# A binary cross-entropy kernel at the DMA limit: reordering VectorE's tail, and sixteen 32-byte writes to the output at launch

## The chip, the core and the metric

The kernel runs on one core of one Trainium2 chip. The metric is the device time of an execution in microseconds (us), as the median over executions. The profile's span is about 2 us shorter than this time (1865.4 against 1867.3 us in the profiled run of the kernel before).

## The reference

```python
pred   = uniform(0.01, 0.99), (8192, 8192), float32
target = 0 or 1,              (8192, 8192), float32
eps = 1e-7
pred = np.clip(pred, eps, 1 - eps)
return -(target * np.log(pred) + (1 - target) * np.log(1 - pred))
```

Two inputs of 268 MB are read and one output of 268 MB is written: 805.3 MB in all, with little work on each element. As target is 0 or 1, the kernel computes -ln|pred + target - 1|.

## The kernel before

The 8192 x 8192 elements are cut into chunks of 128 partitions x up to 15360 columns, two halves of a chunk at the start and at the end, and a last one of 2048 columns. Two rings in SBUF hold them: pred in float32 (in place also the result), target cast to bfloat16 by the load.

```python
def load(k):                       # target by GpSimd's queue, pred too (chunk 0: SP's)
    queue = nc.sync if k == 0 else nc.gpsimd
    nc.gpsimd.dma_start(out=spot(ring_t, k), in_=chunk(target, k))
    queue.dma_start(out=spot(ring_p, k), in_=chunk(pred, k))

def store(k):                      # the last three by SP's queue
    queue = nc.sync if k >= n - 3 else nc.gpsimd
    queue.dma_start(out=chunk(out, k), in_=spot(ring_p, k))

def front(k, *part):
    # VectorE: clip (L82), then (target - 1) + pred (L85); ScalarE: Abs (L88), Ln (L89)
    ...

def back(k, *part):                # VectorE: times -1 (L93)
    ...

# the main part
for k in range(3): load(k)
nc.vector.memset(warm, 1.0)
nc.scalar.activation(out=warm, in_=warm, func=Act.Ln)     # its table load: 1.28 us from 0.73 us
front(0); front(1); back(0); store(0); back(1); store(1); load(3)
for k in range(2, n - 3):
    front(k, (0, 2)); front(k, (1, 2)); back(k, (0, 2)); back(k, (1, 2))
    ...                                                   # store(k), further loads
store(n - 4)
a, b, c = n - 3, n - 2, n - 1      # 7680, 7680 and 2048 columns
front(a); front(b, (0, 2)); front(b, (1, 2))
back(a); store(a); front(c); back(b); store(b); back(c); store(c)
```

(Reformatted and cut; the "..." mark cuts.)

## Time and profile before

| | before |
|---|---|
| time, median of the first 3 runs | 1867.1 us (1866.34 to 1867.97) |
| span in the profile | 1865.4 us |
| busy: VectorE (DVE), ScalarE (ACT), GpSimd (POOL) | 60%, 48%, 3% |
| DMA queues, share of 16 engines | 98.4% and 1.7% |

Here the busy shares of compute tell little: nothing is above 60% but the DMA engines. So the reader should look at the stretches in which a DMA engine stands idle or is slow. Two views serve for this. The windows give each stretch's DMA share and GB/s. The trace's packet records give start, length, queue and bytes of each packet; they carry no engine number, but outside holes one packet starts as another ends, so the records can be threaded into 16 lanes (in the kernel before, 98 of 100 packets then start between 0.019 us before and 0.005 us after the end of the last one in their lane, and none more than 0.02 us before it; so records overlap a little). "An engine" below is such a lane. The prediction shows the lines.

### The profile page before, as it was taken

How to read it: one execution, taken by the hardware profiler on the slowest of the kernel's cores; microseconds unless marked ns; L12 is line 12 of the kernel's file. 1: busy time of each engine (PE TensorE's matmuls, PEld its weight loads, DVE VectorE, ACT ScalarE, POOL GpSimd, SP SyncE). 2: the span in 40 equal slices, each digit the busy share in tenths (PEclk: the TensorE clock that was granted, in tenths of full speed). 3: DMA queues.
4: the chain of work that ended last, by engine and by line, in shares of the span. 5: the costliest groups of instructions: out<-in, count | busy, mean ns of one | idle time of the engine just before them, and what ended most of it. 6: DMA issues, size and time to landing. Idle time of an engine off the chain costs nothing.

```text
span 1865.4 us, 619 instructions
## 1 busy us (share of the span) xinstructions
DVE 1122.2 (60%) x210; ACT 899.9 (48%) x142; POOL 60.9 (3%) x111
## 2 busy tenths in 40 slices
DVE  4655767555576655557665555766555576755575
ACT  3345553335555334555543355553345555433556
POOL 0000000000000000000000000000000000000010
DMA  9999999999999999999999999999999999999998
GB/s 295 376 358 340 357 341 365 387 379 353 344 353 353 359 387 381 351 353 345 353 360 387 385 350 353 345 353 361 383 386 349 354 350 345 362 383 387 356 329 379
DMA packets 15988, 671.13 MB, mean 360 GB/s; under 512 B 1776, under 2 KB 1776, under 8 KB 1904
## 3 DMA queue, kind: packets, MB, share of 16 engines
q0 software_dynamic: 15408, 658.25, 98.4%
q1 hardware_dynamic: 576, 12.85, 1.7%
q14 instruction: 4, 0.03, 0.0%
HBM read 536.87 MB, written 268.44 MB: 432 GB/s over the span
## 4 chain that ended last, share of the span: by engine, by line
DMA 36%; ACT 24%; issue 23%; DVE 16%; POOL 1%; DVEq 0%; POOLq 0%; PEldq 0%
DMA ring_p<-in_pred_dram 33%; ACT ring_p L88 12%; ACT ring_p L89 12%; DVE ring_p L85 8%; DVE ring_p L82 4%; DVE ring_p L93 4%; DMA out_dram<-ring_p 3%; POOL ring_t L73 0%; POOL out_dram L78 0%; DVEq L154 0%; POOLq L78 0%; DVEq L85 0%; PEldq L154 0%; POOLq L74 0%; POOLq L73 0%
## 5 line engine op out<-in xcount | busy, mean ns | idle before, releaser
L88 ACT ACTIVATE ring_p<-ring_p 128x7680 f32<-128x7680 f32 (+1 forms) x70 | 450.6, 6437 | 948.2 <-DVE ring_p L85 948.2
L85 DVE SCALAR_TENSOR_TENSOR ring_p<-ring_t,ring_p 128x7680 f32<-128x7680 bf16 (+1 forms) x70 | 557.2, 7960 | 2.4
L82 DVE TENSOR_SCALAR ring_p<-ring_p 128x7680 f32<-128x7680 f32 (+1 forms) x70 | 284.0, 4057 | 391.0 <-DMA ring_p<-in_pred_dram 391.0
L93 DVE TENSOR_SCALAR ring_p<-ring_p 128x7680 f32<-128x7680 f32 (+1 forms) x69 | 284.0, 4117 | 336.2 <-ACT ring_p L89 336.2
L89 ACT ACTIVATE ring_p<-ring_p 128x7680 f32<-128x7680 f32 (+1 forms) x70 | 451.1, 6444 | 2.2
L78 POOL DMA_DIRECT2D out_dram<-ring_p x34 | 21.6, 635 | 841.0 <-DVE ring_p L93 841.0
L74 POOL DMA_DIRECT2D ring_p<-in_pred_dram x36 | 19.3, 535 | 909.5 <-DMA out_dram<-ring_p 909.5
L73 POOL DMA_DIRECT2D ring_t<-in_target_dram x37 | 20.3, 550 | 0.8 <-PEq L154 0.8
L99 ACT ACT_TABLE_LOAD x1 | 1.3, 1283 | 0.7 <-PEq L143 0.7
L98 DVE MEMSET warm<- 1x8 f32 x1 | 0.1, 65 | 0.8 <-PEq L143 0.8
L99 ACT ACTIVATE warm<-warm 1x8 f32<-1x8 f32 x1 | 0.2, 208 | 0.0
L143 POOL MEMSET const-float32-0.0<- 128x1 f32 x1 | 0.1, 98 | 0.2 <-issue 0.2
L143 POOL MEMSET const-bfloat16-1.0<- 128x1 bf16 x1 | 0.1, 101 | 0.0
L143 POOL MEMSET const-float32-1.0<- 128x1 f32 x1 | 0.1, 98 | 0.0
L143 POOL MEMSET const-uint8-127<- 128x1 uint8 x1 | 0.1, 98 | 0.0
## 6 DMA issues: line engine op xcount, KB each, us to landing
ring_p<-in_pred_dram POOLq DMA_DIRECT2D x32, 7680.0 KB, 35.9
out_dram<-ring_p POOLq DMA_DIRECT2D x32, 7680.0 KB, 29.2
ring_t<-in_target_dram POOLq DMA_DIRECT2D x32, 3840.0 KB, 46.8
ring_p<-in_pred_dram POOLq DMA_DIRECT2D x3, 3840.0 KB, 35.0
ring_t<-in_target_dram POOLq DMA_DIRECT2D x4, 1920.0 KB, 27.6
out_dram<-ring_p POOLq DMA_DIRECT2D x2, 3840.0 KB, 27.6
out_dram<-ring_p SPq DMA_DIRECT2D x2, 3840.0 KB, 12.2
ring_p<-in_pred_dram SPq DMA_DIRECT2D x1, 3840.0 KB, 18.6
```

Of the source, the lines that this page charges most:

```text
L73: nc.gpsimd.dma_start(out=spot(ring_t, k), in_=chunk(target, k))
L74: queue.dma_start(out=spot(ring_p, k), in_=chunk(pred, k))
L78: queue.dma_start(out=chunk(out, k), in_=spot(ring_p, k))
L82: nc.vector.tensor_scalar(out=p, in0=p, scalar1=EPS, scalar2=1 - EPS, op0=Alu.max, op1=Alu.min)
L85: nc.vector.scalar_tensor_tensor(out=p, in0=t, scalar=1.0, in1=p, op0=Alu.subtract, op1=Alu.add)
L88: nc.scalar.activation(out=p, in_=p, func=Act.Abs)
L89: nc.scalar.activation(out=p, in_=p, func=Act.Ln)
L93: nc.vector.tensor_scalar(out=p, in0=p, scalar1=-1.0, scalar2=None, op0=Alu.mult)
L98: nc.vector.memset(warm, 1.0)
L99: nc.scalar.activation(out=warm, in_=warm, func=Act.Ln)
L143: nc = _bacc.Bacc("TRN2", target_bir_lowering=False, num_devices=1)
```

## The change

Its intent: on VectorE, put front(a) ahead of the last back of the chunk before (z), so that ScalarE does not wait for it (16.49 us in the trace); and write 16 runs of 32 bytes to the output at launch, meant as one for each DMA engine, so that a first write's cost, if there is one, is paid early.

```diff
-    warm = pool.tile([1, 8], fp32, name="warm", tag="warm")
+    warm = pool.tile([16, 8], fp32, name="warm", tag="warm")
...
+        nc.vector.memset(warm, 1.0)
+        nc.scalar.dma_start(out=chunk(out, 0)[0 : P : P // 16, : warm.shape[1]], in_=warm)
         for k in range(3):
             load(k)
-        nc.vector.memset(warm, 1.0)
...
-        for k in range(2, n - 3):
+        for k in range(2, n - 4):
...
-        store(n - 4)
-        a, b, c = n - 3, n - 2, n - 1
+        z, a, b, c = range(n - 4, n)
+        front(z, (0, 2))
+        front(z, (1, 2))
+        back(z, (0, 2))
         front(a)
+        back(z, (1, 2))
+        store(z)
         front(b, (0, 2))
```

(Blank lines and the rest of the loop are left out; its test of which stores to issue falls away.)

More of the change, by code (lines that the diff above doesn't have):

```diff
@@ L111 @@
             back(k, (1, 2))
-            if k < n - 4:
-                store(k)
-                for j in range(k + 2, n if k == n - 5 else k + 3):
-                    load(j)
-        store(n - 4)
-        a, b, c = n - 3, n - 2, n - 1
+            store(k)
+            for j in range(k + 2, n if k == n - 5 else k + 3):
+                load(j)
+        z, a, b, c = range(n - 4, n)
+        front(z, (0, 2))
+        front(z, (1, 2))
+        back(z, (0, 2))
         front(a)
+        back(z, (1, 2))
+        store(z)
         front(b, (0, 2))
```

## The prediction

> **What bounds the kernel now.** I read the page first: busy shares, the DMA row of the slices, and the queues.
>
> ```profile
> DVE 1122.2 (60%) x210; ACT 899.9 (48%) x142; POOL 60.9 (3%) x111
> ...
> DMA  9999999999999999999999999999999999999998
> ...
> q0 software_dynamic: 15408, 658.25, 98.4%
> q1 hardware_dynamic: 576, 12.85, 1.7%
> ...
> HBM read 536.87 MB, written 268.44 MB: 432 GB/s over the span
> ```
>
> No compute engine is above 60%, while the two DMA queues together fill the 16 engines' time (98.4% + 1.7%, a little over 100 because records overlap). So the DMA engines are the bound in every slice but the last, and the chain of waits, which names ACT (24%) and DVE (16%), does not contradict this: it follows releases, not capacity. The change moves no fewer bytes, so it can only gain where DMA engines stand idle or a packet takes longer than it should. I went through the trace's DMA packet records one by one. In the steady part a packet of 61440 bytes takes 2.267 us, so 16 engines give 16 x 61440 / 2.267 = 433.6 GB/s. All of the 805.3 MB at that rate is 1857.2 us, against a span of 1865.4 us. **Some 8 us is all that any reordering can address**, 0.44% of the time.
>
> Where are these 8 us? (1) Launch: the first packets start 1.74 to 2.49 us into the span, and the first on each engine takes 1.45 to 2.29 us where the next take 1.14 to 1.17. (2) At 72.6 to 73.4 us the last packet of the load ahead of the first store takes 2.80 to 3.49 us on all 16 engines, on average 0.97 us more than 2.267. The windows (columns: stretch, DVE, ACT, POOL, clock, DMA share, GB/s) show the rate drop there with the share still near 1:
>
> ```profile
> 70.00:72.50 2.50, 0.00 (x0) 0.00 (x0) 1.02 (x2) 1.00 0.91 393
> 72.50:76.00 3.50, 0.00 (x0) 0.00 (x0) 0.00 (x0) 1.00 0.99 307
> 76.00:80.00 4.00, 2.83 (x1) 0.00 (x0) 0.00 (x0) 1.00 1.05 453
> ```
>
> Later starts of a store cost only some engines 0.1 to 0.9 us. They pull the engines apart: one load's landings spread over 0.7 us at the start, 4.4 us from about 460 us on. (3) The tail. The timeline (start, length, what, idle before and its releaser):
>
> ```profile
> 1797.53 6.60 ACT L89 ACTIVATE ring_p<-ring_p 128x7680 f32<-128x7680 f32 x1
> 1804.17 4.16 DVE L93 TENSOR_SCALAR ring_p<-ring_p 128x7680 f32<-128x7680 f32 x1 [8.97 <-ACT ring_p L89]
> 1808.24 4.15 DVE L82 TENSOR_SCALAR ring_p<-ring_p 128x7680 f32<-128x7680 f32 x1
> 1808.62 3.90 POOL L78 DMA_DIRECT2D out_dram<-ring_p  x1 [22.23 <-DVE ring_p L93]
> 1812.43 8.16 DVE L85 SCALAR_TENSOR_TENSOR ring_p<-ring_t,ring_p 128x7680 f32<-128x7680 bf16 x1
> ...
> 1820.62 6.61 ACT L88 ACTIVATE ring_p<-ring_p 128x7680 f32<-128x7680 f32 x1 [16.49 <-DVE ring_p L85]
> ...
> 1838.08 14.93 SPq L78 DMA_DIRECT2D out_dram<-ring_p  x3
> ```
>
> DVE waits 8.97 us for ScalarE before back(z, second half), although chunk a is in SBUF by 1801.6 (its landing records). ScalarE then waits 16.49 us for front(a). Everything after is late: the store of b cannot be issued before its negation ends at 1851.51. The windows show what the DMA loses:
>
> ```profile
> 1844.00:1848.00 4.00, 0.65 (x1) 4.00 (x2) 0.00 (x0) 1.00 0.96 415
> 1848.00:1850.00 2.00, 2.00 (x1) 1.97 (x2) 0.00 (x0) 1.00 0.36 154
> 1850.00:1852.00 2.00, 2.00 (x2) 1.06 (x1) 0.00 (x0) 1.00 0.04 15
> 1852.00:1854.00 2.00, 0.65 (x1) 0.00 (x0) 0.00 (x0) 1.00 1.17 492
> ```
>
> Between 1848 and 1852.4 the engines run dry one after another: eight at 1848.1 to 1848.7, the last at 1851.5. All restart at 1852.4 and end together at 1864.0 to 1864.2. The gap is up to 4.4 us on the engines that are ahead, but **only 0.84 us on the engine that is behind**.
>
> [...]the issue at 1808.62 took 3.90 us instead of the usual 0.54 and ended 0.13 us after the tensor_scalar that ran over it.[...]
>
> **The change, part by part.**
>
> Part 1, the tail. I redo the timeline with the new order: front(z), back(z, first), front(a), back(z, second), store(z), front(b), back(a), store(a), front(c), back(b), store(b), back(c), store(c). Durations are from the timeline (7680 columns: tensor_scalar 4.16, subtract-add 8.16, each activation 6.6; half of it for 3840 columns: 2.15, 4.16, 3.4). front(a) starts at 1801.6 when a lands, and ends at 1801.6 + 12.4 = 1814.0, 6.6 us before 1820.6. back(z, second) follows to 1818.2, 9.9 us later than now, and store(z) is issued then. It must be: the loads of c end on the engines between 1820.3 and 1824.6, so store(z) still arrives in time, and no tensor_scalar covers its issue, as b lands only at 1819.8. ScalarE does a from 1814.1 to 1827.3 (before: 1820.6 to 1833.9). front(b) runs on DVE from 1819.8 to 1832.4; ScalarE does b from 1827.3 to 1840.9 (before: to 1847.3). back(a) ends at 1836.6, so store(a) goes out 1.4 us earlier; front(c) ends at 1840.1, back(b) at 1845.1 and store(b) goes out there, 6.4 us earlier than 1851.5. DMA needs it from 1848.1 at the earliest: the gap closes on all engines. But the end is the last engine's. The one that is behind gets 0.84 us back; those ahead finish some 4 us sooner, which nobody sees. **Part 1: -0.8 us**, though compute is 6.4 us earlier.
>
> Part 2, the launch write. The most plausible reading of the 0.97 us at 72.6 us is a price of an engine's first write to the output. It is on all engines, and the next store's start shows only 0.1 to 0.35 us on four. A 32-byte write at launch pays it early. The memset ends at 0.87 us; the SP issue at 0.74 has its first packet at 1.74, so one on ScalarE's queue at about 0.9 has its own at about 1.9 to 2.0, while each engine is in its slow first load packet (0.3 to 1.1 us over the usual). If the two overlap, 1.0 us is saved; if they add, the loss only moves from 73 us to 2 us and nothing is saved. I take 0.6 us. **Part 2: -0.6 us.**
>
> Other additions are hidden: the wider memset is a single short instruction; the warm-up activation must wait for the little write to have read its source, some microseconds, but ScalarE has nothing else to do before 31.7 us; the store of chunk 0 may have to wait for the little write, done 50 us earlier.
>
> Sum: 1867.1 - 0.8 - 0.6 = 1865.7 us.
>
> **Rivals.**
> (A) The gap of 4.4 us counts in full: the end moves by all that the windows show idle, about 4 us, plus 1, to 1862. For it: the windows' 0.36 and 0.04. Against it: the per-engine times, with the last engine dry for 0.84 us only. It would need the spread of 4.4 us among engines to shrink too, for instance because the launch write changes how they drift apart.
> (B) The launch write adds its price at launch and loads are late by up to 1 us; with the tail that gives 1866.3. For it: the DMA engines are busy without a break from 1.74 us on, so any stall after that counts. Against it: the first packets are slow anyhow.
> (C) The later store(z) becomes a new wait: should b land before back(z, second) ends, a tensor_scalar of 2.15 us blocks its issue on GpSimd, and the engines ahead run dry at 1820. Their slack of 4.4 us covers this; only if the issue slips beyond 1824.6 does the end move. It would be 1867 to 1869. The margin of 1.6 us at 1818.2 speaks against it.
> (D) The drift among engines settles elsewhere: the engine behind has lost some 4 us against the one ahead in small stalls between 128 and 730 us. Another pattern moves the end by 1 to 2 us either way.
>
> **Range and chances.** The three times before span 1.6 us, half the effect or more is of that size, and (D) adds the same again. I take 1863.6 to 1867.3: the lower end is part of (A), the upper is no gain at all. Two per cent are 37 us; there is not a quarter of that to gain, and a loss of that size would need a transfer held up for most of a chunk, of which I see no cause. Faster 0.005, same 0.985, slower 0.01.
>
> **What would show it.** Right: the packets at about 72 us take 2.27 us on all engines; the first two packets of each engine lose no more than now; ScalarE's 16.49 us wait before a is some 10 us; front(a) stands before the last back of z; store(z) is issued near 1817 to 1819; store(b) near 1844 to 1845; no window between 1846 and the end has a share far under 0.9 until the engines that are ahead finish, about 4 us before the last. Wrong: the long packets stay at 72 us (the price is not that of a first write), or move to the launch (B); store(z)'s issue takes over 2 us (C); all engines end together and earlier than 1861 (A). A time under 1863 would say that the spread shrank, one above 1868 that the new order starves DMA.

No term of the sum is cut: it came to 1867.1 - 0.8 - 0.6 = 1865.7 us. The -0.8 is worked out from the trace's 0.84 us; the -0.6 is the author's estimate, between nothing and the 1.0 us (0.97 in the trace) that would be saved in full. That each engine would get one of the 16 runs, between two of its load packets, was not shown before the result. That 433.6 GB/s is a ceiling was not shown either: it is the rate of the steady packets, and the 8 us are what is lost against it. That a tensor_scalar holds back an issue on GpSimd rests on the one instance at 1808.62.

## More of the kernel before

The rounds of runs were on different chips, each beside runs of the kernel before, whose medians lie between 1867.0 and 1867.5 us.

Across a hole, in which several lanes stand idle, a lane cannot be followed; only the times at which lanes end and start again are sure.

## The result

| | before | after |
|---|---|---|
| time, median of 6 runs each | 1867.5 us (1866.34 to 1868.11) | 1866.41 us (1865.92 to 1866.57) |
| ratio | | 0.9994, 95% interval 0.9981 to 1.0007 |
| span in the profile | 1865.4 us | 1864.3 us |

A ratio is the mean time of one kernel's runs over that of the other's of the same rounds, so it is not quite the ratio of the medians. The difference of 1.1 us is below what the interval can tell from zero; what makes it credible is that the packet records show it, too, in every profile: the last landing is at 1864.3 and 1864.6 us in the two kernels with the old tail, at 1862.8 to 1863.4 in the changed kernel, e1, e3, e4 and e8, which have the new one.

The page of the changed kernel, the same lines as those of before:

```profile
DVE 1122.2 (60%) x210; ACT 899.9 (48%) x142; POOL 57.5 (3%) x111
...
DMA  9999999999999999999999999999999999999999
...
q0 software_dynamic: 15408, 658.25, 98.5%
...
q10 hardware_dynamic: 32, 0.00, 0.0%
HBM read 536.87 MB, written 268.44 MB: 432 GB/s over the span
```

The last slice of the DMA row went from 8 to 9. The launch write is there as queue q10: 16 packets of 32 bytes, each of 9 ns, and 16 of 4 bytes, which end at 5.87 to 6.62 us, before the 16 semaphore updates of the write's landing (6.19 to 6.96 us). Each of the 32-byte packets starts within 0.01 us of the end of one load packet and the start of the next, all 16 in 0.76 us, less than the shortest of these load packets takes (1.14 us): so there was one on each of the 16 engines, between two of its load packets. GpSimd has 3.4 us less, as the issue of store(z), with no tensor_scalar over it, took 0.54 us in place of 3.90. Its timeline in the tail (start, length, what, idle before):

```profile
1801.74 4.16 DVE L82 TENSOR_SCALAR ring_p<-ring_p 128x7680 f32<-128x7680 f32 x1 [6.54 <-DMA ring_p<-in_pred_dram]
1805.93 8.16 DVE L85 SCALAR_TENSOR_TENSOR ring_p<-ring_t,ring_p 128x7680 f32<-128x7680 bf16 x1
1814.01 4.15 DVE L93 TENSOR_SCALAR ring_p<-ring_p 128x7680 f32<-128x7680 f32 x1
1814.13 6.60 ACT L88 ACTIVATE ring_p<-ring_p 128x7680 f32<-128x7680 f32 x1 [9.99 <-DVE ring_p L85]
1818.46 0.54 POOL L78 DMA_DIRECT2D out_dram<-ring_p  x1 [32.03 <-DVE ring_p L93]
...
1836.57 9.95 SPq L78 DMA_DIRECT2D out_dram<-ring_p  x3
...
1840.86 5.30 DVE L93 TENSOR_SCALAR ring_p<-ring_p 128x7680 f32<-128x7680 f32 x2 [0.85 <-ACT ring_p L89]
```

front(a) now starts at 1801.74 us, 0.1 us after a lands (1801.64), ScalarE's wait is 9.99 us in place of 16.49, and the negations of b and c are done at 1846.2 us; before, they ended at 1852.6. The three stores on SP's queue are all issued within 9.95 us where it took 14.93. The windows of the end (stretch, DVE, ACT, POOL, clock, DMA share, GB/s):

```profile
1844.00:1848.00 4.00, 2.15 (x2) 0.57 (x1) 0.00 (x0) 1.00 1.05 453
1848.00:1850.00 2.00, 0.00 (x0) 0.00 (x0) 0.00 (x0) 1.00 0.96 415
1850.00:1852.00 2.00, 0.00 (x0) 0.00 (x0) 0.00 (x0) 1.00 0.93 399
1852.00:1854.00 2.00, 0.00 (x0) 0.00 (x0) 0.00 (x0) 1.00 1.14 492
...
1858.00:1862.00 4.00, 0.00 (x0) 0.00 (x0) 0.00 (x0) 1.00 0.72 305
1862.00:1865.00 3.00, 0.00 (x0) 0.00 (x0) 0.00 (x0) 1.00 0.05 22
```

The hole at 1848 to 1852 us (shares 0.36 and 0.04 before) is gone on all engines. But the idle time has moved to the end: the engines now finish between 1860.2 and 1863.1 us, where all ended at 1864.0 to 1864.2 before. The last packet ends 1.1 us earlier; the engines that are ahead finish almost 4 us earlier, and nobody needs them.

The windows at the first turn from loads to stores look as before:

```profile
70.00:72.50 2.50, 0.00 (x0) 0.00 (x0) 1.08 (x2) 1.00 0.91 393
72.50:76.00 3.50, 0.00 (x0) 0.00 (x0) 0.00 (x0) 1.00 0.99 325
76.00:80.00 4.00, 2.76 (x1) 0.00 (x0) 0.00 (x0) 1.00 1.02 438
```

The rate still falls (to 325 GB/s, 307 before), and in the packet records all 16 packets that start at 72.8 to 73.6 us are long, by 0.84 us on average (0.97 before). This is within what differs between runs of one kind, as the table under the stall experiments shows. The launch write has not removed the stall.

### The profile page after: what moved, and what is told of

The parts are those of the page before. It is cut to its first block, busy times and chain, and to the rows that moved or that the text cites. A ratio compares the mean times of both kernels' runs of the same rounds, so it can differ in the third digit from the quotient of the medians.

```text
span 1864.3 us, 622 instructions
## 1 busy us (share of the span) xinstructions
DVE 1122.2 (60%) x210; ACT 899.9 (48%) x142; POOL 57.5 (3%) x111
## 4 chain that ended last, share of the span: by engine, by line
DMA 35%; issue 26%; ACT 22%; DVE 15%; POOL 1%; DVEq 0%; POOLq 0%; PEldq 0%
DMA ring_p<-in_pred_dram 32%; ACT ring_p L88 11%; ACT ring_p L89 11%; DVE ring_p L85 7%; DVE ring_p L82 4%; DVE ring_p L93 4%; DMA out_dram<-ring_p 3%; POOL ring_t L73 0%; POOL out_dram L78 0%; DVEq L160 0%; POOL ring_p L74 0%; POOLq L78 0%; POOLq L73 0%; DVEq L82 0%; PEldq L160 0%
## 6 DMA issues: line engine op xcount, KB each, us to landing
ring_p<-in_pred_dram SPq DMA_DIRECT2D x1, 3840.0 KB, 18.7
```

## The experiments

Three questions: which part gives the 1.1 us; whether the end really is that of the engine behind; and what the stall at 73 us is, if not the price of a first write. Twelve kernels ran, all with correct results (the number e6 is not used on the record). A launch write is placed before the store of the same bytes (in the changed kernel it had landed by 6.96 us, and that store was issued at 56.7), so it does not show in the output.

### Each part alone

**e1_tail_only**: the changed kernel without the launch write.

```diff
-        nc.scalar.dma_start(out=chunk(out, 0)[0 : P : P // 16, : warm.shape[1]], in_=warm)
```

(The memset went back to its old place and size.)

> The new tail order without the launch write. Theory: all of the gain of 1.1 us is the tail, since in the changed kernel the 16 long packets at 73 us are still there (mean excess 0.84 us against 0.97): ratio 0.9994 to 0.9995, about 1 us under before, and the last landing near 1863.4. Rival (the launch write gives half of it): 0.5 us under before or less. Packets at 73 us long on all 16 engines either way.

Measured: 1865.97 us (5 runs) beside 1867.19 of before (9 runs), ratio 0.9994 (0.9980 to 1.0008); last landing 1863.41 us (1863.44 with both parts, 1864.56 before); 16 long packets at 73 us.

**e2_launch_only**: the kernel before with the launch write.

```diff
+        nc.vector.memset(warm, 1.0)
+        nc.scalar.dma_start(out=chunk(out, 0)[0 : P : P // 16, : warm.shape[1]], in_=warm)
         for k in range(3):
```

> The launch write without the new tail. Theory: no gain, ratio 0.9999 to 1.0002, with the long packets at 73 us on all engines (excess 0.8 to 1.0) and the DMA gap at 1848 to 1852 as in before. Rival: 0.5 us faster or more.

Measured: 1867.31 us (5 runs) beside the same 1867.19, ratio 1.0002 (0.9989 to 1.0014); 16 long packets at 73 us; last landing 1864.31 us. Its windows have the old hole:

```profile
1848.00:1850.00 2.00, 2.00 (x1) 1.97 (x2) 0.00 (x0) 1.00 0.36 154
1850.00:1852.00 2.00, 2.00 (x2) 0.83 (x1) 0.00 (x0) 1.00 0.04 15
```

So the tail gives all of the gain that the landings show, and the launch write none that these runs can see. It costs nothing visible either: pred 0 landed at 18.65 to 19.52 us with the write, at 18.56 to 19.53 in e1_tail_only without it.

### Is the end that of the engine behind?

**e8_late_b5** and **e9_late_b10**: the changed kernel with multiplications of b by 1.0 on VectorE, which hold back its store and change no value.

```diff
         front(c)
+        q = spot(ring_p, b, (0, 1))      # e8: all of b once (e9: twice)
+        nc.vector.tensor_scalar(out=q, in0=q, scalar1=1.0, scalar2=None, op0=Alu.mult)
+        q = spot(ring_p, b, (0, 4))      # e8: then its first quarter (e9: its first half)
+        nc.vector.tensor_scalar(out=q, in0=q, scalar1=1.0, scalar2=None, op0=Alu.mult)
         back(b)
```

> The changed kernel with the store of b held back by multiplications by 1.0 on VectorE, about 5.3 us: issue near 1850.4 in place of 1845.1. The engines ahead run dry for 1 to 2 us, the one behind does not. Theory (the end is that of the engine behind): time within 0.3 us of the changed kernel. Rival (idle time of the engines counts in the mean or in full): 1 to 2 us longer.

> The same with about 10.4 us of multiplications: issue near 1855.5, first packets near 1856.4, after the engine behind has run dry at about 1851.9. Theory: the end moves by what that engine waits, 3.5 to 5 us over the changed kernel, and all engines end together within 0.3 us.

The windows of e8_late_b5:

```profile
1848.00:1850.00 2.00, 2.00 (x1) 0.00 (x0) 0.00 (x0) 1.00 0.22 92
1850.00:1852.00 2.00, 1.33 (x2) 0.00 (x0) 0.00 (x0) 1.00 0.64 276
```

and of e9_late_b10:

```profile
1848.00:1850.00 2.00, 1.97 (x2) 0.00 (x0) 0.00 (x0) 1.00 0.39 169
1850.00:1852.00 2.00, 1.97 (x2) 0.00 (x0) 0.00 (x0) 1.00 0.00 0
1852.00:1854.00 2.00, 2.00 (x1) 0.00 (x0) 0.00 (x0) 1.00 0.00 0
1854.00:1858.00 4.00, 2.21 (x2) 0.00 (x0) 0.00 (x0) 1.00 0.58 246
```

Measured: e8 1866.25 us, ratio to before 0.9996 (0.9984 to 1.0009); e9 1871.45 us, ratio 1.0024 (1.0011 to 1.0038); before 1867.05 in these rounds. In e8 fourteen engines run dry for 0.7 to 2.9 us and two not at all: the end does not move (last packet 1862.9 us; 1863.1 in the changed kernel). In e9 the engine with the least dry time has 4.9 us and the last packet ends at 1867.8 us, 4.7 later than in the changed kernel. In this tail each engine still has the same work to do after the hole (in the kernel before, 16 packets in each lane). There the pair shows the rule in both directions: **the dry time of the engine that has the least of it is what the end pays**, to within the 0.6 us by which last landings differ anyhow; not the mean, and not what the windows show. Rival (A) of the prediction, the gap in full, falls with it.

### What is the stall at 73 us?

For every run, the excess over 2.267 us (2.281 for target loads) of the packets around the first turn from loads to a store, summed over the 16 engines, from the packet records; the spread is that of the landings of pred 1, before the turn:

```text
kernel            excess (engine-us)   long packets   spread (us)
before                 15.5                16            0.7
after                  13.4                16            0.8
e1_tail_only           14.5                16            1.0
e2_launch_only         15.1                16            0.9
e3_write_gpsimd        15.5                16            0.9
e4_write_2kb           11.5                16            0.8
e5_target3_first       17.6 (at 89-92)     20            0.8
e8_late_b5             16.7                16            0.9
e9_late_b10            12.7                16            0.9
e12_stagger_half       19.4                16            1.5
e10_stagger_own        14.7                21            2.7
e11_early_c            15.9                18            2.9
e13_stagger_two        13.6                25            4.9
e7_stagger              0.0                 0            3.9
```

**e3_write_gpsimd**: the 32-byte write on the queue of the first store. **e4_write_2kb**: 128 rows of 2 KiB, meant as 8 on each engine, as the 128 rows of pred 0 are 8 packets in each lane of the kernel before.

```diff
-        nc.scalar.dma_start(out=chunk(out, 0)[0 : P : P // 16, : warm.shape[1]], in_=warm)
+        nc.gpsimd.dma_start(out=chunk(out, 0)[0 : P : P // 16, : warm.shape[1]], in_=warm)   # e3
+        early = ring_p[:, 2 * BIG : 2 * BIG + 512]                                            # e4
+        nc.vector.memset(early, 1.0)
+        nc.scalar.dma_start(out=chunk(out, 0)[:, :512], in_=early)
```

> The changed kernel with its 32-byte launch write issued from GpSimd, the queue of the first store. If the price at 73 us is that of the first write on that queue, the packets at 73 us take 2.27 us and the excess is under 0.2 us. If it is not bound to the queue, the excess stays 0.8 to 1.0 us on all engines. I expect the second.

> The launch write made real: 128 rows of 2048 bytes, 8 on each engine, in place of 16 runs of 32 bytes (some 0.7 us of DMA more at launch). If the price at 73 us belongs to an engine's first write of ordinary size, the excess there falls under 0.2 us and the time is about that of the changed kernel. If it belongs to all engines turning from loads to stores at the same moment, the excess stays 0.8 to 1.0 us and the time is 0.5 to 1 us over the changed kernel.

(The 0.7 us of added DMA is an estimate: on a line through the trace's 0.309 us for 8192 bytes and 2.267 us for 61440, 2048 bytes take 0.083 us, eight of them 0.66.)

Measured: e3 1866.31 us (one look), e4 1866.40 us (4 runs, ratio 0.9995, 0.9982 to 1.0009). In both the stall stays on all engines. So it is neither a price of the first write to the output, nor of the first write on that queue, nor of a first write of more than 32 bytes. A full-size first write on the store's own queue was not tried ahead of time; but e7, below, makes its first store without a long packet. e4's 11.5 is the least of the table but for e7's, but one run does not make that a partial effect, as 12.7 to 16.7 come without any such write. That e4 would be 0.5 to 1 us slower was a miss; it was not.

**e5_target3_first**: the target of chunk 3 loaded ahead of the first store.

```diff
         back(0)
+        nc.gpsimd.dma_start(out=spot(ring_t, 3), in_=chunk(target, 3))
         store(0)
...
-        load(3)
+        nc.gpsimd.dma_start(out=spot(ring_p, 3), in_=chunk(pred, 3))
```

> The changed kernel with the target of chunk 3 loaded ahead of the first store, so that the first turn from loads to a store comes 18 us later. If the long packets belong to the first turn from load to store, they move from 73 us to about 92 us, on all engines, and at 73 us packets take 2.27 us. If they belong to that point in time (or to that load), they stay at 73 us. The time is 2 to 3 us longer, since the issue of pred 3 now waits for the second store with nothing queued behind it.

Measured: 1870.80 us (one look). No packet at 73 us is long; 20 packets from 88.7 to 91.7 us are. The stall goes with the first turn from loads to a store, not with a time or a certain load. Two more stalls follow: 12.0 engine-us at 116 us, which is no such turn but the first packets of a load after the queue had run empty, and 17.3 at the next turn at 132 us. The time was 4.4 us over the changed kernel, where 2 to 3 were expected.

**e7_stagger**: if all engines turning at once is the cause, parting them must help. One more load at launch, on 8 engines only.

```diff
+        nc.scalar.dma_start(out=ring_p[0:8, BIG : 2 * BIG], in_=chunk(pred, 2)[0:8, :])
```

> The changed kernel with one added load at launch of 8 rows of 61440 bytes (overwritten later by the real load), which holds 8 of the 16 engines back by one packet, 2.27 us. If the stalls come from all engines turning from loads to stores in the same moment, the summed excess at 73 to 76 us falls to half or less of 15 engine-us, and the spread of about 3.3 us hardly grows over the run: last landing within 0.5 us of the changed kernel's 1863.4 or earlier, though 8 engines move one packet more. If each engine pays for its first store by itself, the excess stays 13 to 15 engine-us, the drift of 3 us comes on top, and the end is 1.5 to 2.3 us later.

Measured: 1870.79 us (4 runs, ratio 1.0020, 1.0006 to 1.0034), so slower; yet no long packet at the first turn, and four in all from there to the tail (the spread grows from 3.9 us only to 4.3). The windows at its first turn, 5 us later than in the changed kernel, keep the rate:

```profile
76.00:78.50 2.50, 2.28 (x1) 0.00 (x0) 0.00 (x0) 1.00 1.08 467
78.50:82.00 3.50, 0.00 (x0) 0.00 (x0) 1.08 (x2) 1.00 1.01 439
```

The time was lost at launch. The 8 added packets took 7.1 to 8.6 us each in place of 2.27, and pred 0 landed at 24.1 to 27.9 us (18.7 to 19.5 in the changed kernel). All eight together took 9.3 us (7.96 to 17.27), less than two in a row would take, so they ran on eight engines, and their 8 x 61440 bytes came at 53 GB/s; at 2.27 us each it would be 217. pred 0 was 5.4 to 8.5 us later although only these 8 packets were added: even its first engine landed 4.6 us after the last one of the changed kernel. From that landing on, the engine behind ran 8.4 us later than in the changed kernel but finished only 4.5 later: 4 us of stalls were not there. Summed from 30 us to the tail, packets that are too long cost 33 engine-us in the kernel before and 1 in e7. That looked like a kernel worth having, if the stagger came cheaply.

**e10_stagger_own**, **e11_early_c**, **e12_stagger_half**, **e13_stagger_two**: the stagger on the tail-only kernel, with the rows of a transfer on partitions 4 apart (0, 4, ... 28 in e10 and e12) in place of 0 to 7.

```diff
+        nc.scalar.dma_start(out=ring_p[0:32:4, BIG : 2 * BIG], in_=chunk(pred, 2)[0:32:4, :])             # e10
+        nc.scalar.dma_start(out=ring_p[0:32:4, BIG : BIG + HALF], in_=chunk(pred, 2)[0:32:4, :HALF])      # e12
+        for m in range(2):                                                                                # e13
+            nc.scalar.dma_start(out=ring_p[m : m + 29 : 4, BIG : 2 * BIG], in_=chunk(pred, 2)[m : m + 29 : 4, :])
+        for m in (0, 1, 2, 3, 32, 33, 34, 35):                                                            # e11
+            nc.scalar.dma_start(out=spot(ring_p, n - 1)[m : m + 29 : 4], in_=chunk(pred, n - 1)[m : m + 29 : 4])
```

(In e11 the later load of pred c keeps only partitions 64 to 127.)

> The tail-only kernel with the staggering load of before, now with 8 rows that lie in the partitions 0, 4, ... 28[...]; in the first stagger run these rows were partitions 0 to 7, each such packet took 7.1 to 8.6 us and the start lost 5.4 to 8.5 us. If that was the cost, the packets take about 2.3 us, the engines part by 2.3 to 3 us at the first landing, the excess at 73 us falls under 3 engine-us and the drift stops; last landing near 1861.7 and time near 1864.7, 1.0 to 1.7 us under the tail-only kernel. If the stagger does not help, the added packet costs 1 to 2 us over the tail-only kernel.

> The tail-only kernel with half of the last pred chunk (partitions 0 to 63, in 8 transfers of 8 rows of 8192 bytes) loaded at launch by 8 engines in place of the end: a stagger of 8 x 0.31 = 2.5 us without an added byte. If the stagger is what stops the stalls, excess at 73 us under 3 engine-us, spread 2.5 to 3.5 us over the whole run, last landing 1860.7 to 1862, time 1863.7 to 1865. If not, time as the tail-only kernel or up to 2.5 us longer.

Measured: e10 1869.97 us (ratio 1.0017, 1.0003 to 1.0030), e11 1869.22 us (1.0014, 1.0001 to 1.0026), before 1867.14. The added packets of e10 took 2.27 us each, so the partitions 0 to 7 are the likely cost in e7; the rows that are read from HBM changed with them, and e7 had the launch write besides; no run parts these. But the stall at 73 us stayed, and stalls of 12 to 14 engine-us came again later (at 237 and 510 us in e10; at 291, 510 and 619 us in e11). From 30 us to the tail the long packets sum up to 71 and 67 engine-us, twice those of the kernel before. Both are slower than it, and by more than the expectations gave for a stagger that does not help (4.0 and 3.3 us over e1_tail_only, where 1 to 2 and at most 2.5 were foretold): the hoped-for version does not exist in this form. In e10 the eight engines behind all have a long packet at their own turn (0.2 to 1.2 us), and five of them one before it, in their last but one load, while the engines ahead turn: a part of the price is paid before the engine's own turn.

> The tail-only kernel with 8 rows of 30720 bytes added at launch on 8 engines: half a packet, 1.14 us. If what matters is where in the 2.27 us of a packet the engines stand to each other (one whole packet[...] left them all in the same 0.8 us of it and the stall stayed), half a packet spreads them over it: excess at 73 us under 4 engine-us and time 1 to 2 us under the tail-only kernel. If what matters is the spread in us (3.8 in the run without stalls, 2.7 in those with), the spread of 1.9 us is too small: excess 12 to 16 engine-us, time equal to the tail-only kernel or up to 2.5 us longer.

> The tail-only kernel with 16 rows of 61440 bytes added at launch on 8 engines: two packets, 4.5 us. If the place within a packet matters, the engines are again in step and the excess at 73 us stays 12 to 16 engine-us. If the spread in us matters, 5.3 us is enough, the excess falls under 4 engine-us and no stall on all engines follows; last landing then near 1864 (the engines behind carry 4.5 us more and lose nothing), time 0.5 to 1 us over the tail-only kernel. If neither, time 3 to 5 us over it.

Measured: e12 1868.67 us (1.0007, 0.9993 to 1.0020), e13 1869.53 us (1.0016, 1.0002 to 1.0029), before 1866.99. Half a packet and two packets both leave the stall. So neither the place within a packet nor the spread in us explains by itself why e7 has none. Nor is it enough that its added load held back the issue of pred 2 by 16.8 us (in e13 15.1 us), or that its second store was issued only 2.2 us before the first landing of pred 2 (78.6 against 80.8 us; 6.1 us in the changed kernel, but 1.8 in e13). Two differences were not parted: e7 kept the launch write, which e10 to e13 do not have, and only its added packets were slow. **What makes e7 free of stalls stays open**, and with it the cause of the stalls. What the runs do show: nearly all of the large stalls come at turns from loads to stores (e5's at 116 us does not), the first such turn costs 11 to 19 engine-us in 13 of 14 kernels (0.7 to 1.2 us of all 16 engines), and in e10 some engines pay a part before their own turn.

No version beat the changed kernel clearly; e1_tail_only equals it with less code.

## Why the prediction was right

The time, 1866.41 us, lies in the range of 1863.6 to 1867.3 and 0.7 us over the 1865.7 foretold, but one of the two terms of the sum was wrong. The range says little: its upper end, 1867.3, is no gain at all, so that a change that does nothing would have lain in it, too. That the sum came out near is in part luck; the mechanism is right for the tail and wrong for the launch write.

- **The bound.** Nothing speaks against it: no run came below 1865.3 us, and nothing that was tried won more than some 1 us of the 8.
- **Part 1, the schedule of the tail.** Right to about 0.3 us at each point: front(a) 1801.7 (foretold 1801.6), last back of z to 1818.2 (1818.2), store(z) issued 1818.5 in 0.54 us with no instruction over it, a on ScalarE from 1814.1 (1814.1), negations of b and c to 1846.2 (1845.1 for b and 1.2 for c: 1846.3). Rival (C) did not come true.
- **Part 1, its worth.** -0.8 was foretold; e1_tail_only's median is 1.2 us below that of before, and the last packet ends 1.1 us earlier. The term was a little too small: after its hole, the kernel before restarted its engines between 1852.37 and 1852.52 us, and the second packet of each took 1.19 to 1.20 us in place of 1.14. If the engine behind was also the last to restart, 0.84 + 0.15 + 0.05 = 1.04 of the 1.1 us; that is an account by size alone, since lanes cannot be followed across the hole and kernels with the same tail differ by up to 0.6 us in the last landing. (By the same records nine engines, not eight, had run dry by 1848.7 us; nothing rests on it.) That the 4.4 us of the engines ahead are worth nothing was the step that decided, and e8 and e9 show it.
- **Part 2, the launch write.** Wrong. The step that failed is "the most plausible reading of the 0.97 us at 72.6 us is a price of an engine's first write to the output". The -0.6 us did not come: e2_launch_only is 0.1 us above before, and the stall stayed with 32 bytes, with 2 KiB rows and on the store's own queue. The inference from "all engines, and less at the next turn" to "first write" was the fault; "first turn from loads to stores" fits the same lines, and e5 speaks for it, though e7 shows that such a turn can also be free, and the cause stays open. The place of the write in time was off, too: its packets started at 4.7 to 5.5 us, not at 1.9 to 2.0. Rival (B) also failed: the write cost nothing visible at launch.
- **Rival (D)**, another pattern of drift: it happens (the spread settles at 3.7 us in the changed kernel, 4.4 in before, 3.2 to 4.2 in e1, e2, e4, e8 and e9) but moved the last landing by 0.6 us at most (1862.8 in e4, 1863.3 to 1863.4 in after, e1, e3 and e8).

So the sum was nearly right because a missing 0.6 us was partly made up by 0.3 to 0.4 us more from the tail, which is luck and not foresight.

## What to carry to other kernels

Where the DMA engines are the bound and all have the same work left, find for each hole in the windows the engine that stands idle least; in this tail only that much was won by filling it, and compute that finished 6.5 us sooner was worth 1.1 us. Before paying early for a "first time" cost, move the event that is supposed to be the first and see whether the cost moves with it. A DMA on few partitions is worth a look at which ones: eight rows on partitions 0 to 7 took 7.1 to 8.6 us each in e7, three to four times as long as eight others on partitions 0, 4, ... 28 in e10 (2.27 us), and the traffic beside them was late (pred 0 by 5.4 to 8.5 us).
